# Sharing the first load of a 180-degree rotation between two DMA queues: by rows instead of by columns

## The chip, the cores and the metric

The kernel runs on one core of a Trainium2 chip. The metric is the time of one execution on the device in microseconds (us). The work is nearly all transfer: images are read from HBM into the core's SBUF (128 partitions), turned there by VectorE, and written back to HBM. Transfers are issued by an engine's instruction stream (SyncE or ACT here), each of which has a queue of its own, and are carried out by the core's 16 DMA engines.

## What is computed

```python
batch, c, h, w = 32, 3, 256, 256
x = np.random.randn(batch, c, h, w).astype(np.float32)

def reference(x):
    return np.rot90(x, k=2, axes=(-2, -1)).astype(np.float32)
```

Each of the 96 images is rotated by 180 degrees. Seen as one line of 65,536 numbers, an image is simply reversed. 25.17 MB are read and as many written.

## The kernel before

The 96 images are taken in three groups of 32. An image is cut into four quarters of E = 16,384 numbers (64 KB), and a group's 32 x 4 quarters are laid on the 128 partitions, one quarter to a partition. Row r of `x4[g]` is thus 64 KB that lie together in HBM, and goes to partition r. Three tiles `A`, `Bt` and `Ct` hold one group each, so that all three loads can be issued at once; a fourth, `T`, of J = 2,048 columns, is scratch.

The rotation has two parts. Within a quarter the numbers are reversed in SBUF by VectorE: `swap` (lines 61 to 65) exchanges a stretch of columns with its mirror image, by three copies, each of them reading backwards where needed: the right stretch into `T`, the left one to the right place, and `T` to the left place. `inside` (lines 67 to 69) does this for a whole tile in four swaps of 2,048 columns. The order of the four quarters of an image is reversed by the store (lines 57 to 59), which writes them in the order `::-1`. All copies are VectorE's, at line 52, held in program order.

What is issued, in order:

- The loads (line 55). `A`'s first 512 columns, 2 KB of each row, go on ACT's queue (line 72); its other 15,872 columns, 62 KB of each row, on SyncE's (line 73). Then SyncE issues the loads of `Bt` and `Ct`, 64 KB of each row (lines 74 and 75).
- VectorE turns `A` but for the middle: three swaps of 2,048 columns and one of 896 (lines 78 to 80). SyncE stores `A`'s first 128 columns, 64 KB in all (line 81).
- VectorE turns `Bt` (line 82), then the middle of `A`, 1,152 columns (line 83).
- SyncE stores the rest of `A` (line 84) and `Bt` (line 85). VectorE turns `Ct` (line 86), and SyncE stores it (line 87).

All stores and all loads but one are on SyncE's queue, where they are carried out in the order of issue. A semaphore for each transfer tells when it has landed; the waits are set by the framework from the regions that each instruction reads and writes. VectorE's first copy for a tile waits for its load, and SyncE's store waits for VectorE's last copy of what it stores.

Of the kernel before, what the change touches and what calls it, by code (L numbers as in the profile page):

```python
# [2 lines left out]

os.environ.setdefault("NEURON_RT_ULTRASERVER_MODE", "4")

# [4 lines left out]


@with_exitstack
def kernel(
    ctx: ExitStack,
    tc: tile.TileContext,
    x: bass.AP,
    out: bass.AP,
):

    nc = tc.nc
    P = 128

    B, C, H, W = x.shape
    L = H * W
    G = 32
    E = L // 4
    J = E // 8

    x4 = x.rearrange("b c h w -> (b c) (h w)").rearrange(
        "(g n) (s e) -> g (n s) e", n=G, s=4)
    o4 = out.rearrange("b c h w -> (b c) (h w)").rearrange(
        "(g n) (s e) -> g n s e", n=G, s=4)  # L40

    pool = ctx.enter_context(tc.tile_pool(name="slots", bufs=1))
    A = pool.tile([P, E], x.dtype, tag="A")
    Bt = pool.tile([P, E], x.dtype, tag="B")
    Ct = pool.tile([P, E], x.dtype, tag="C")
    T = pool.tile([P, J], x.dtype, tag="T")

    def back(t, lo, hi):
        return t[:, hi - 1:(lo - 1 if lo else None):-1]

    def copy(dst, src):
        tc.keep_in_program_order(nc.vector.tensor_copy(out=dst, in_=src))  # L52

    def load(t, g, lo, hi, queue=nc.sync):
        return queue.dma_start(out=t[:, lo:hi], in_=x4[g][:, lo:hi])  # L55

    def store(t, g, lo, hi):
        return nc.sync.dma_start(
            out=o4[g][:, ::-1, lo:hi], in_=t[:, lo:hi])

    def swap(t, lo, w):
        hi = E - lo - w
        copy(T[:, 0:w], back(t, hi, hi + w))
        copy(t[:, hi:hi + w], back(t, lo, lo + w))
        copy(t[:, lo:lo + w], T[:, 0:w])

    def inside(t):
        for lo in range(0, E // 2, J):
            swap(t, lo, J)

    HEAD = 512
    load(A, 0, 0, HEAD, nc.scalar)
    load(A, 0, HEAD, E)
    load(Bt, 1, 0, E)
    load(Ct, 2, 0, E)
    LAST = 1152
    LEAD = 128
    for lo in range(0, E // 2 - J, J):
        swap(A, lo, J)
    swap(A, E // 2 - J, J - LAST)  # L80
    store(A, 0, 0, LEAD)
    inside(Bt)
    swap(A, E // 2 - LAST, LAST)
    store(A, 0, LEAD, E)
    store(Bt, 1, 0, E)
    inside(Ct)
    store(Ct, 2, 0, E)


# [1 line left out]
_INS = ['x']  # L91
_OUTS = [((32, 3, 256, 256), 'float32')]


# [23 lines left out]
```

## Time and profile before

| | us |
|---|---|
| median of 3 runs | 121.94 (121.89 to 122.06) |
| the profiled execution | 122.03 |
| its span, from the first instruction to the last | 120.2 |
| VectorE (DVE) busy | 44.6, in 39 instructions |
| DVE's first copy starts | 22.68 |
| SyncE issues the large store of A | 59.62 |
| SyncE issues the store of Ct | 76.63 |

The profile of one execution gives, for each compute engine, its busy time, and a strip that cuts the span into 40 slices and shows each slice's busy share in tenths. Issuing a transfer isn't counted as busy. A row for each DMA queue says how many packets it carried, how many MB, and which share of the 16 DMA engines' time they took. A packet is what one DMA engine moves in one go; here it is one row of one transfer, and each transfer adds 16 packets of 4 bytes that signal its end. Times of an issue "to landing" run from the issuing instruction to the signal that all of it is there. Where a wait is listed, the engine, its tile and line stand first, then what ended the wait, the total, the number of times, and the longest.

### The profile page before, as it was taken

To read this page: it belongs to the slowest core of one execution; us is meant where nothing else is said; L and a number is where in the kernel's file an instruction comes from. 1 tells how busy PE (TensorE), PEld (TensorE's weight loads), DVE (VectorE), ACT (ScalarE), POOL (GpSimd) and SP (SyncE) were. 2 spreads that over 40 slices of the span, in tenths; PEclk is the share of its full clock that TensorE was granted. 3 is DMA by queue.
4 is the path that set the end of the run, shared out by engine and by line. 5 is a ranking of instruction groups with operands and counts; after the bars stand their busy time and mean duration, and the time that the engine had idled before them with its cause. 6 is when DMAs were issued, how large, how long until landed. Compare 5 with 4: busy or idle time off the path is not lost.

```text
span 120.2 us, 98 instructions
## 1 busy us (share of the span) xinstructions
DVE 44.6 (37%) x39; POOL 0.2 (0%) x4
## 2 busy tenths in 40 slices
DVE  0000000499990099999759999400000000000000
POOL 0000000000000000000000000000000000000000
DMA  9888988899889988998889777988898889888980
GB/s 338 349 349 349 698 349 349 360 654 392 349 349 610 436 349 349 589 458 349 349 368 692 346 346 346 692 349 349 349 698 349 349 349 698 349 349 349 676 371 0
DMA packets 1152, 50.33 MB, mean 419 GB/s; under 512 B 128, under 2 KB 256, under 8 KB 384
## 3 DMA queue, kind: packets, MB, share of 16 engines
q1 hardware_dynamic: 1008, 50.07, 96.7%
q10 hardware_dynamic: 144, 0.26, 0.6%
HBM read 25.17 MB, written 25.17 MB: 419 GB/s over the span
## 4 chain that ended last, share of the span: by engine, by line
DMA 34%; DVE 27%; another core or an unknown queue 2%; issue 1%; SPq 0%; DVEq 0%
DMA Bt<-in_x_dram 34%; DVE T L52 9%; DVE Bt L52 8%; DVE Ct L52 8%; DVE A L52 1%; SPq L55 0%; DVEq L52 0%
## 5 line engine op out<-in xcount | busy, mean ns | idle before, releaser
L52 DVE COPY T<-A 128x2048 f32<-128x2048 f32 (+2 forms) x5 | 5.1, 1014 | 22.8 <-DMA A<-in_x_dram 22.7
L52 DVE COPY T<-Bt 128x2048 f32<-128x2048 f32 x4 | 4.9, 1227 | 6.2 <-DMA Bt<-in_x_dram 6.1
L52 DVE COPY T<-Ct 128x2048 f32<-128x2048 f32 x4 | 4.9, 1227 | 2.0 <-DMA Ct<-in_x_dram 1.9
L52 DVE COPY A<-T 128x2048 f32<-128x2048 f32 (+2 forms) x5 | 5.1, 1013 | 0.2
L52 DVE COPY A<-A 128x2048 f32<-128x2048 f32 (+2 forms) x5 | 5.1, 1013 | 0.2
L52 DVE COPY Bt<-T 128x2048 f32<-128x2048 f32 x4 | 4.9, 1227 | 0.1
L52 DVE COPY Ct<-T 128x2048 f32<-128x2048 f32 x4 | 4.9, 1227 | 0.1
L52 DVE COPY Bt<-Bt 128x2048 f32<-128x2048 f32 x4 | 4.9, 1226 | 0.1
L52 DVE COPY Ct<-Ct 128x2048 f32<-128x2048 f32 x4 | 4.9, 1226 | 0.1
L102 POOL MEMSET const-bfloat16-1.0<- 128x1 bf16 x1 | 0.1, 103 | 0.0
L102 POOL MEMSET const-uint8-127<- 128x1 uint8 x1 | 0.1, 103 | 0.0
L102 POOL MEMSET const-float32-1.0<- 128x1 f32 x1 | 0.1, 100 | 0.0
L102 POOL MEMSET const-float32-0.0<- 128x1 f32 x1 | 0.1, 99 | 0.2 <-issue 0.2
## 6 DMA issues: line engine op xcount, KB each, us to landing
out_dram<-A SPq DMA_DIRECT2D x1, 8128.0 KB, 21.2
A<-in_x_dram SPq DMA_DIRECT2D x1, 7936.0 KB, 21.9
A<-in_x_dram ACTq DMA_DIRECT2D x1, 256.0 KB, 22.1
out_dram<-A SPq DMA_DIRECT2D x1, 64.0 KB, 35.2
Bt<-in_x_dram SPq DMA_DIRECT2D x1, 40.8
Ct<-in_x_dram SPq DMA_DIRECT2D x1, 59.8
out_dram<-Bt SPq DMA_DIRECT2D x1, 39.9
out_dram<-Ct SPq DMA_DIRECT2D x1, 42.8
```

The lines of the kernel that those rows point to most:

```text
L52: tc.keep_in_program_order(nc.vector.tensor_copy(out=dst, in_=src))
L102: nc = _bacc.Bacc("TRN2", target_bir_lowering=False, num_devices=1)
```

## The change

The two loads of `A` are cut in another way. Before, both touch all 128 rows: ACT's takes 2 KB of each row, SyncE's the other 62 KB. After, each takes 64 whole rows of 64 KB: SyncE's the even rows to the even partitions, ACT's the odd ones. SyncE's half stands first in the program. Nothing else differs.

```diff
-    HEAD = 512
-    load(A, 0, 0, HEAD, nc.scalar)
-    load(A, 0, HEAD, E)
+    SPLIT = 2
+    for i in range(SPLIT):
+        (nc.sync, nc.scalar)[i % 2].dma_start(
+            out=A[i::SPLIT, :], in_=x4[0][i::SPLIT, :])
     load(Bt, 1, 0, E)
     load(Ct, 2, 0, E)
```

## The prediction

> **What bounds the kernel now.** I read the page's strip of slices first, because it says at once whether an engine or the transfers set the time, then its queue table, then the issues with their landings, then the waits, and last the start of the span in small stretches.
>
> ```profile
> span 120.2 us, 98 instructions
> ...
> DVE 44.6 (37%) x39; POOL 0.2 (0%) x4
> ...
> DMA  9888988899889988998889777988898889888980
> ...
> q1 hardware_dynamic: 1008, 50.07, 96.7%
> q10 hardware_dynamic: 144, 0.26, 0.6%
> HBM read 25.17 MB, written 25.17 MB: 419 GB/s over the span
> ```
>
> VectorE (DVE) works 37% of the span, while the 16 DMA engines are busy in every slice but the last. q1 is SyncE's queue, q10 is ACT's. Together they hold the engines for 97.3% of the span, so about 3.2 us are left in which no transfer runs, most of them at the two ends: the first packet starts at 1.77 us, the last ends at 119.09. A change to the load can gain only by a cheaper packet, by an earlier first packet, or lose by opening a hole.
>
> ```profile
> A<-in_x_dram SPq DMA_DIRECT2D x1, 7936.0 KB, 21.9
> A<-in_x_dram ACTq DMA_DIRECT2D x1, 256.0 KB, 22.1
> ...
> Bt<-in_x_dram SPq DMA_DIRECT2D x1, 40.8
> Ct<-in_x_dram SPq DMA_DIRECT2D x1, 59.8
> ```
>
> The last column is the time from issue to landing. SyncE issues at 0.73, 1.18 and 1.65 us (timeline), so A is there at 22.8, Bt at 42.0 and Ct at 61.4: one group per 19.3 us, in a row, with nothing between. The packet records (each DMA packet's start and length) give the beat behind it. A 64 KB packet takes 2.418 us, and each engine starts the next one 2.4145 us after the last; a group is eight such rounds of 16 packets, 8 x 2.4145 = 19.32 us. In A's load a round is one 62 KB packet (2.342 us) and one 2 KB packet (0.084 us), and rounds follow at 2.419 us. The next two lines are the queue rows of the stretch from 4.75 to 7.15 us, one such round:
>
> ```profile
> q1 hardware_dynamic: 16, 1.02, 97.6%
> q10 hardware_dynamic: 16, 0.03, 3.5%
> ```
>
> Each engine takes one packet of SyncE's queue and one of ACT's in turn. That is why ACT's 256 KB, issued at 0.73, land only at 22.8 with the rest.
>
> The reader must also see who waits for A:
>
> ```profile
> DVE T L52 <- DMA A<-in_x_dram: 22.7, 1, 22.7
> DVE T L52 <- DMA Bt<-in_x_dram: 6.1, 1, 6.1
> DVE T L52 <- DMA Ct<-in_x_dram: 1.9, 1, 1.9
> ```
>
> Having finished its part of A, DVE waits 6.1 us for Bt. So A may land up to 6.1 us later and DVE is still in time for Bt. Behind Bt there is no such room: the chain from Bt's landing (42.0) through 12 copies of 1.23 us and three of 0.76 us ends at 59.6, the large store of A is issued at 59.62, and its first packets start at 60.82, when the first engines have just run out of loads (60.45) and of the eight 512-byte packets behind them (0.027 us each, so 60.7). Loads and this chain are level within 0.15 us. Both begin at the same place, the landing of the loads, so an earlier or later first round moves both and the end with them, one for one.
>
> **The change, part by part.**
>
> Bytes, issues and rounds. Two loads of A go (62 KB and 2 KB of each row), two come (64 whole rows each). SyncE still issues A, Bt, Ct and ACT one load, in parallel. Packets: 128 of 62 KB and 128 of 2 KB become 128 of 64 KB, half on each queue. Per engine that is 4 + 4 instead of 8 + 8. A round of A falls from 2.419 to 2.4145 us; over eight rounds -0.036 us. No work hides it, since the engines are the bound.
>
> Sharing. The round shown above alternates the queues packet by packet, so I take even, odd, even, odd on each engine, and A complete after eight rounds as now. If a queue ran ahead by a packet or two, A would land 2.4 to 4.8 us later, with Bt's first packets moved before it; Bt's end stays, because the bytes ahead of it are the same, and DVE's 6.1 us cover A. Cost nothing; without the cover it would be the excess over 6.1.
>
> DVE's first copy. It now needs both loads (before, only SyncE's; the second copy needed ACT's). Behind it stand all other copies, and SyncE's first store. A few hundredths of a us, covered by the same 6.1.
>
> The first round is the only term that could be seen. The stretches at the start (length, DVE, POOL, clock, DMA engines' share, GB/s booked where a packet starts):
>
> ```profile
> 1.50:2.00 0.50, 0.00 (x0) 0.00 (x0) 1.00 3.89 1270
> 2.00:2.50 0.50, 0.00 (x0) 0.00 (x0) 1.00 1.00 381
> 2.50:3.00 0.50, 0.00 (x0) 0.00 (x0) 1.00 0.90 381
> 3.00:4.75 1.75, 0.00 (x0) 0.00 (x0) 1.00 0.00 0
> ```
>
> 1270 GB/s over 0.5 us is ten packets of 62 KB, 381 is three. So ten engines begin by 2.0 us and the other six straggle to 2.89 us, while SyncE's issue has ended at 1.12. The early ten need 3.0 to 3.4 us for this packet, the late ones down to 2.34. All end between 4.78 and 5.27 us, and this spread of 0.49 us stays to the end of the loads (58.03 to 58.52 for the last round's starts). The slowest engine sets the landings, so what counts is the 5.27. Before, two loads of 128 rows are being turned into packets at that time; after it is two of 64, half the packets, and I guess that the six stragglers come from that work. The trace does not show it. Bounds: at best every engine ends its first packet at the earliest 4.78, -0.49 us. At worst the issue itself gets dearer: a load's issue takes 0.38 to 0.43 us, a store's, with its reordered rows, 0.54 to 0.63, so +0.25 us for rows with a step. I take the stragglers falling in with the early ten, whose last ends at 5.16: -0.11 us. It is the row nearest to the change, since nothing in it alters what the ten show.
>
> [...]
>
> Sum: -0.036 - 0.11 = -0.15 us. The profiled execution took 122.03 us, its span 120.2 and 1.8 around it; it becomes 121.88. It lies 0.09 above the median of the three runs (121.94), so against the median the forecast is 121.79, or **121.8 us**. About 0.2% (0.24 us) is what a measurement of this kernel can tell from no change, so the forecast is "the same".
>
> **The rivals.**
>
> *Faster, about 121.55.* The stragglers come wholly from the doubled packet work and the early ones' long first packets too; the first round ends near 4.9 us. -0.036 - 0.35 = -0.39 us. For it: the late six start while three further loads are being issued. Against it: 128 of the 256 packets removed are small, and Bt's and Ct's loads stay.
>
> *Slower: ACT's load waits for SyncE's, about 125.1.* Even and odd rows interleave in the same tile. If whoever sets the waits takes them for one overlapping region, ACT may issue only when the even rows have landed: 5.27 + 3 x 2.41 = 12.5, plus 0.4 until a wait is over (Bt: 41.6 last packet, 42.0 seen) and 1.0 from issue to first packet, 13.9. On each engine a Bt packet is then under way until 14.9; four odd ones alternating with three of Bt end at 14.9 + 7 x 2.41 = 31.8 instead of 22.3. DVE starts A 9.5 us later. 6.1 are covered, 3.4 are not: Bt's copies start at 45.5, A's last copy ends at 63.0, and its store's packets start at 64.2, when the engines have been out of work since 61.3. The end moves by about 3.2 us. It decides from the point where A is over 6.1 us late. Against it: before, the two parts of A's rows were kept apart rightly (both issue at 0.73).
>
> *Slower by the start, about 122.2.* The stepped rows make SyncE's and ACT's issue as dear as a store's, +0.25, with nothing won back.
>
> *The change doesn't do what it says: 64 rows don't fill 16 engines.* All transfers of the trace have 128 rows. Were a load of 64 rows to run at half the rate, A's eight rounds would last as long as sixteen, +19.3 us, 141.2. Against: 64 rows divide by 16 engines as 128 do. [...]
>
> **How the numbers follow.** Within 0.2%: 0.41, nearly all of it the forecast. Faster by more: 0.33, the first rival and the bound of the start. Slower by more: 0.26, made of 0.12 for a dearer or less lucky start, 0.10 for ACT's wait, 0.04 for half rate. The range takes in both bounds of the start: 121.94 - 0.036 - 0.49 = 121.41 and 121.94 + 0.25 = 122.19, each with about 0.1 more for the spread of the runs shown (121.89 to 122.06): 121.3 to 122.35. What it leaves out is the two dear cases, 0.14, and some chance beyond the ends.
>
> **What would show it.** In the profile after: 64 KB packets only in A's rounds, 8 on each queue in a round of 16, and rounds at 2.4145 us; ACT's issue still at 0.73 (if it is near 12.9, ACT waits); first packets all begun by about 2.5 us and ended by 5.16; A at about 22.6, Bt at 41.9; DVE's wait for Bt near 6.1. If A's rounds are longer than 2.42 us, the sharing of engines is wrong. If the first packets straggle as before or more, the term of the start is wrong, and only the 0.04 stands.

## The result and the profile after

The changed kernel takes 122.56 us (median of 9 runs, 122.27 to 123.07), the kernel before 122.00 in the runs beside it (9 runs, 121.89 to 122.32). The ratio is 1.0046, with a 95% interval from 1.003 to 1.0061: slower by about 0.56 us, clear of no change. The profiled execution took 122.66 us.

The page of the profile after, in the rows that were shown of before:

```profile
span 120.9 us, 97 instructions
...
DVE 44.6 (37%) x39; POOL 0.2 (0%) x4
...
DMA  8988998899889988998889877988898889888980
...
q1 hardware_dynamic: 944, 46.14, 88.3%
q10 hardware_dynamic: 80, 4.19, 8.5%
```

The picture is the same: the transfer engines are busy in all slices but the last, and VectorE does what it did. ACT's queue now carries 4.19 MB. The two queues hold 96.8% of a longer span; before it was 97.3%. In the packet records the last packet ends at 119.72 us instead of 119.09, so the 0.6 us lie before it. The timeline of the changed kernel shows where they begin (start, length, engine, line):

```profile
0.73 0.58 SPq L73 DMA_DIRECT2D A<-in_x_dram  x1
0.73 0.53 ACTq L73 DMA_DIRECT2D A<-in_x_dram  x1
1.36 0.81 SPq L55 DMA_DIRECT2D Bt<-in_x_dram  x1
2.21 0.44 SPq L55 DMA_DIRECT2D Ct<-in_x_dram  x1
```

The same issues before:

```profile
0.73 0.38 ACTq L55 DMA_DIRECT2D A<-in_x_dram  x1
0.73 0.39 SPq L55 DMA_DIRECT2D A<-in_x_dram  x1
1.18 0.43 SPq L55 DMA_DIRECT2D Bt<-in_x_dram  x1
1.65 0.43 SPq L55 DMA_DIRECT2D Ct<-in_x_dram  x1
```

The issues of A's halves have become dearer, that is longer, by 0.19 us on SyncE and 0.15 on ACT. The stretches at the start (the last column is GB/s, booked where a packet starts; a 64 KB packet in half a microsecond is 131):

```profile
1.50:2.00 0.50, 0.00 (x0) 0.00 (x0) 1.00 0.00 0
2.00:2.50 0.50, 0.00 (x0) 0.00 (x0) 1.00 4.69 1573
2.50:3.00 0.50, 0.00 (x0) 0.00 (x0) 1.00 0.75 262
3.00:3.50 0.50, 0.00 (x0) 0.00 (x0) 1.00 0.60 262
```

Where before ten engines began by 2.0 us, none does: twelve begin between 2.0 and 2.5, two in each stretch after it. By the packet records the first packet starts at 2.07 us (before 1.77), the last engine's first at 3.39 (2.89), and the slowest engine ends its first packet at 5.99 (5.27). Before, a 2 KB packet of 0.084 us still belonged to that round, so the slowest engine began its second round at 5.35, now at 5.99: 0.64 us later. From there on the delay is carried along:

```profile
DVE T L52 <- DMA A<-in_x_dram: 23.5, 1, 23.5
DVE T L52 <- DMA Bt<-in_x_dram: 5.8, 1, 5.8
DVE T L52 <- DMA Ct<-in_x_dram: 1.9, 1, 1.9
```

DVE gets A at 23.5 us instead of 22.7 and still waits 5.8 for Bt. Bt's copies start at 42.68 instead of 42.10, the large store of A is issued at 60.19 instead of 59.62, and the end is later by the same 0.6.

Sixteen packets of a stretch from 7.40 to 9.83 us, the third round, show the sharing, with ACT's queue first:

```profile
q10 hardware_dynamic: 16, 1.05, 99.6%
```

In the round before it all 16 were SyncE's, in the next they are again. Rounds of A follow at 2.416 us.

### The profile page after: what moved, and what is told of

The parts are those of the page before. It is cut to its first block, busy times and chain, and to the rows that moved or that the text cites. A ratio compares the mean times of both kernels' runs of the same rounds, so it can differ in the third digit from the quotient of the medians.

```text
span 120.9 us, 97 instructions
## 1 busy us (share of the span) xinstructions
DVE 44.6 (37%) x39; POOL 0.2 (0%) x4
## 3 DMA queue, kind: packets, MB, share of 16 engines
q10 hardware_dynamic: 80, 4.19, 8.5%
## 4 chain that ended last, share of the span: by engine, by line
DMA 34%; DVE 26%; another core or an unknown queue 1%; issue 1%; SPq 0%; DVEq 0%
DMA Bt<-in_x_dram 34%; DVE T L52 9%; DVE Bt L52 8%; DVE Ct L52 8%; DVE A L52 1%; SPq L73 0%; DVEq L52 0%
## 5 line engine op out<-in xcount | busy, mean ns | idle before, releaser
L52 DVE COPY T<-A 128x2048 f32<-128x2048 f32 (+2 forms) x5 | 5.1, 1014 | 23.7 <-DMA A<-in_x_dram 23.5
## 6 DMA issues: line engine op xcount, KB each, us to landing
A<-in_x_dram SPq DMA_DIRECT2D x1, 22.7
```

## The experiments

Two theories could stand after this profile. **STEP**: rows with a step between them are dear to turn into packets. **QUEUES**: two loads of equal weight on two queues hold each other up. A third, **ROWS**, that a load of 64 rows is dear for itself, is told apart by the first run. All kernels are edits of the kernel before unless said otherwise, and ratios are to it.

### e1_halves

```diff
-    load(A, 0, 0, HEAD, nc.scalar)
-    load(A, 0, HEAD, E)
+    nc.sync.dma_start(out=A[0:64, :], in_=x4[0][0:64, :])
+    nc.scalar.dma_start(out=A[64:128, :], in_=x4[0][64:128, :])
```

> SyncE loads rows 0 to 63 of A, ACT rows 64 to 127: 64 rows each as in the changed kernel, but without a step between rows. Theory STEP (rows with a step are dear to turn into packets): issues back at 0.38 to 0.43 us, first packets ended by 5.3 us, time 122.0. Theory ROWS (64 rows of 64 KB on each of two queues start late, stepped or not): issues at 0.53 to 0.58, first packets ended only near 6.0, time 122.5. [...]

Measured: 142.17 us, ratio 1.1659 [1.1643, 1.1675]. The start first, from the timeline of this run:

```profile
0.73 0.59 SPq L71 DMA_DIRECT2D A<-in_x_dram  x1
0.73 0.53 ACTq L72 DMA_DIRECT2D A<-in_x_dram  x1
1.37 0.80 SPq L55 DMA_DIRECT2D Bt<-in_x_dram  x1
```

There is no step between the rows, and the issues are as dear as in the changed kernel; the first packet starts at 2.07 us here too. STEP is out. Then the 20 us. The head and the queue row of a stretch from 6.7 to 11.6 us, one round of A:

```profile
DMA packets 16, 1.05 MB, mean 214 GB/s; under 512 B 0, under 2 KB 0, under 8 KB 0
...
q1 hardware_dynamic: 16, 1.05, 100.4%
```

All 16 engines work the whole stretch, at half the rate: a 64 KB packet takes 4.92 us instead of 2.42. A's rounds follow at 4.913 us, so the seven after the first cost 7 x (4.913 - 2.419) = 17.46 us more. The first ends 2.30 later (7.57 instead of 5.27), the late start included, and Bt's first packets still take 2.8 to 3.3 us. The slowest engine begins Bt's second round at 44.76 instead of 24.70, 20.06 us later, and the profiled executions differ by 20.03: that is the loss. From Bt's second round on, packets are back at 2.42. "64 rows don't fill the engines", one of the prediction's rivals with 19.3 us, is real for a block of rows and absent for every second row. e12_spread, below, finds on which side of the transfer it lies.

### e2_sync_only

```diff
-    load(A, 0, 0, HEAD, nc.scalar)
-    load(A, 0, HEAD, E)
+    load(A, 0, 0, E)
```

> SyncE loads A alone, in one load of 128 rows of 64 KB; ACT issues nothing. Theory STEP: a start like that of the kernel before, first packets ended by 5.3 us, 122.0. Theory QUEUES (two loads that are turned into packets at once hold each other up): a better start than the kernel before, first packets ended before 5.2, 121.8 or less.

Measured: ratio 1.0004 [0.9995, 1.0013], first issue 0.39 us, first packet at 1.75 (before 1.77). One load alone isn't measurably quicker to start than two, so the old 2 KB load on ACT neither helped nor harmed measurably, and QUEUES gets no support. The first packets have all ended only at 5.62 us, later than either theory expected. That is the profiled execution alone, which took 122.28 us, the longest of this kernel's eleven runs; their median is 122.04.

### e3_both_on_sync

```diff
-    load(A, 0, 0, HEAD, nc.scalar)
-    load(A, 0, HEAD, E)
+    for i in range(2):
+        nc.sync.dma_start(out=A[i::2, :], in_=x4[0][i::2, :])
```

> Even rows and odd rows as in the changed kernel, but both loads on SyncE, one behind the other. Theory STEP: issues of 0.53 us or more each, first packets ended near 6.0 us, 122.5. Theory QUEUES: the two no longer meet, issues back at about 0.4 us, first packets ended by 5.3, 122.0.

Measured: ratio 1.0042 [1.0029, 1.0055]; issues of 0.58 us each, first packet at 2.11 us, first packets ended by 5.65, between the two values expected. Without a second queue the loss is the same within the intervals. QUEUES falls.

### e4_columns

```diff
-    load(A, 0, 0, HEAD, nc.scalar)
-    load(A, 0, HEAD, E)
+    load(A, 0, 0, E // 2)
+    load(A, 0, E // 2, E, nc.scalar)
```

> SyncE loads columns 0 to 8191 of all 128 rows of A, ACT the other half: 32 KB of each row on each queue, no step, 128 rows. Theory STEP: issues of 0.38 us, first packets begun by 2.9 us, 122.0. Theory QUEUES in the form that two big loads of equal weight are worse than a big one and a small one: begun late, up to 3.4 us, 122.5.

Measured: ratio 1.0005 [0.9993, 1.0016]; issues 0.38 and 0.40, first packet at 1.74. Two queues with an equal share were no harm here, where each load has 128 rows.

What was left was ROWS, sharpened: the issue of a load of fewer than 128 rows takes longer, the first packet comes later by that and a little more, and nothing else is lost. If so, the loss must vanish where the dear issue lies under other transfers.

### e5_rows_behind

```diff
-    load(A, 0, 0, HEAD, nc.scalar)
-    load(A, 0, HEAD, E)
+    load(A, 0, 0, E // 2)
+    for i in range(2):
+        (nc.sync, nc.scalar)[i].dma_start(
+            out=A[i::2, E // 2:E], in_=x4[0][i::2, E // 2:E])
```

> SyncE loads the left half of A's columns for all 128 rows first; the right half follows by even rows on SyncE and odd rows on ACT. Theory ROWS (a load of 64 rows takes 0.2 us longer to issue and its packets start 0.3 us later; nothing else is dear about it): the 128-row load starts the engines at 1.75 us, the others are issued while they work, 122.0. Rival PACKETS (64-row loads cost in transit, by uneven engines or longer rounds): slower than before by 0.2 to 0.4%.

Measured: ratio 1.0000 [0.9988, 1.0012]. The issues of A's loads, from the timeline:

```profile
0.73 0.37 SPq L55 DMA_DIRECT2D A<-in_x_dram  x1
0.73 0.52 ACTq L73 DMA_DIRECT2D A<-in_x_dram  x1
1.16 0.56 SPq L73 DMA_DIRECT2D A<-in_x_dram  x1
```

The 64-row loads take 0.52 and 0.56 us to issue, as dear as ever, but the engines have begun at 1.73 us with the first load.

### e6_four

```diff
-    load(A, 0, 0, HEAD, nc.scalar)
-    load(A, 0, HEAD, E)
+    for i in range(4):
+        (nc.sync, nc.scalar)[i % 2].dma_start(
+            out=A[i::4, :], in_=x4[0][i::4, :])
```

> A by every fourth row: four loads of 32 rows, two on SyncE and two on ACT. ROWS with a cost for each load that isn't of 128 rows: first packets again at 2.07 us, so 122.5, not more, since the second load on each queue is issued under cover. Were the step between rows the cause, a step of four would be at least as dear, 122.5 or more.

Measured: ratio 1.0033 [1.0021, 1.0045]; first issues of 0.54 (ACT) and 0.58 us (SyncE), first packet at 2.06. Half as many rows and twice the step cost the same within the intervals, and only once.

### e7_rows_of_Bt

```diff
-    load(Bt, 1, 0, E)
+    for i in range(2):
+        nc.sync.dma_start(out=Bt[i::2, :], in_=x4[1][i::2, :])
```

> The kernel before, with Bt loaded by even and odd rows, both on SyncE, behind A. ROWS: Bt's two issues take 0.58 us each but lie under A's load, 122.0. PACKETS: the same 0.3 to 0.5% slower as with A's rows.

Measured: ratio 1.0006 [0.9997, 1.0014]. Bt's two issues take 0.56 and 0.60 us, under A's load. Bt's loads of even and of odd rows cost nothing measurable in transit.

### e8_later_loads

```diff
+    nc.vector.memset(Bt[:, 0:4096], 0.0)
     load(Bt, 1, 0, E)
```

> The kernel before, but VectorE first fills 4,096 columns of Bt with zeros (overwritten by the load), so that SyncE issues Bt and Ct only some 2 to 5 us into the span. If the six late engines at the start come from the issue of Bt and Ct, as the prediction guessed of the packet work, all first packets begin by 2.1 us and have ended by 5.1, and the time is 121.7. If not, the six stay late and the time is 122.0.

Measured: ratio 1.0011 [1.0002, 1.002]. Bt is now issued at 5.15 us, and the stretches of the start read:

```profile
1.50:2.00 0.50, 0.35 (x1) 0.00 (x0) 1.00 5.40 1778
2.00:2.50 0.50, 0.50 (x1) 0.00 (x0) 1.00 0.73 254
2.50:3.00 0.50, 0.50 (x1) 0.00 (x0) 1.00 0.00 0
```

Fourteen engines begin by 2.0 us and the other two by 2.5 (before: ten, three and three up to 2.89). In this profile the stragglers are gone with the issue of the next loads. That they come from it is not shown, though, since two later profiles speak against it. In e9_reordered Bt and Ct are issued at 1.43 and 2.04 us, and all 16 engines begin within 0.32 us; in e11_after_later Bt is issued at 5.15, and one engine begins only at 3.02. And nothing is won here: the first packets still end between 4.67 and 5.35 us (before 4.78 and 5.27), since each of the 16 takes 2.9 to 3.5 us, where the last four to begin took 2.34 to 2.49 before. The whole is slower by about 0.1%, barely clear of no change; the record doesn't say why.

### e9_reordered

```diff
-    load(A, 0, 0, HEAD, nc.scalar)
-    load(A, 0, HEAD, E)
+    x5 = x.rearrange("b c h w -> (b c) (h w)").rearrange(
+        "(g n) (s e) -> g n s e", n=G, s=4)
+    nc.sync.dma_start(out=A[:, :], in_=x5[0][:, ::-1, :])
```

> A in one load of 128 rows on SyncE, ACT issues nothing, but the four quarters of each image are read in reverse order, as the stores write them. The quarters of A's images end up in the order of the input, so the output is not the reference's for these 32 images. Theory ISSUE (whatever makes the first issue dear delays the first packet, and the end follows; the number of rows is only one such thing): issue 0.54 us or more, first packet at 2.05 us, 122.3. If only loads of less than 128 rows are dear: issue 0.39, first packet at 1.75, 122.0.

Measured: ratio 1.0031 [1.0019, 1.0042]. The first issue, from the timeline:

```profile
0.72 0.65 SPq L73 DMA_DIRECT2D A<-in_x_dram  x1
```

And the stretches of the start:

```profile
1.50:2.00 0.50, 0.00 (x0) 0.00 (x0) 1.00 0.00 0
2.00:2.50 0.50, 0.00 (x0) 0.00 (x0) 1.00 6.34 2097
```

The kernel beside it is e2_sync_only, the same one load with its rows in order: issue 0.39, first packet at 1.75, ratio 1.0004. One load of all 128 rows, on one queue, without a step that leaves rows out, loses 0.3% as soon as its issue is dear. No engine begins before 2.0 us, the first at 2.16, and A's rounds follow at 2.415 us, so nothing is lost behind the start. What the kernels that lose have in common is a long first issue and a late first packet; few rows are one way to get them. So ROWS becomes **ISSUE**.

### e10_head_first

```diff
     HEAD = 512
-    load(A, 0, 0, HEAD, nc.scalar)
-    load(A, 0, HEAD, E)
+    load(A, 0, 0, HEAD)
+    for i in range(2):
+        (nc.sync, nc.scalar)[i].dma_start(
+            out=A[i::2, HEAD:E], in_=x4[0][i::2, HEAD:E])
```

> SyncE first loads 512 columns of all 128 rows of A (2 KB of each), then the even rows of the rest; ACT loads the odd rows of the rest. ISSUE: the small load starts the engines at 1.75 us and keeps each busy for 8 x 0.084 = 0.67 us, longer than the 0.3 us that 64-row packets come late, so 122.0 to 122.1. If 64-row loads cost by something else, 122.4 to 122.6.

Measured: ratio 1.0002 [0.9994, 1.0011]. The issues of A's loads, from the timeline:

```profile
0.72 0.38 SPq L55 DMA_DIRECT2D A<-in_x_dram  x1
0.73 0.52 ACTq L74 DMA_DIRECT2D A<-in_x_dram  x1
1.17 0.57 SPq L74 DMA_DIRECT2D A<-in_x_dram  x1
```

The rows are shared as in the changed kernel, with the dear issues and all, but 256 KB of cheap issue stand in front, and their packets run from 1.73 us on. The loss is gone. This is the change, repaired; it is level with the kernel before and no better.

### e11_after_later

The edit is one of the changed kernel:

```diff
+    nc.vector.memset(Bt[:, 0:4096], 0.0)
     load(Bt, 1, 0, E)
```

> The changed kernel, with VectorE first filling 4,096 columns of Bt with zeros, so that SyncE issues Bt and Ct some 4.4 us later. ISSUE explains 0.31 us (first packet at 2.07 instead of 1.77) of the 0.56 lost. If the rest comes from Bt's issue (0.81 us in the changed kernel) falling into the first round, its ends come in from 5.99 to about 5.6 and the time is 122.3; if not, 122.55.

Measured: ratio 1.0039 [1.0026, 1.0053]; the slowest first packet ends at 5.83 us, between the two values expected, and the interval holds 1.0046, the ratio of the changed kernel. Whether Bt's issue of 0.81 us adds to the loss of the changed kernel is not settled by it.

### e12_spread

```diff
-    load(A, 0, 0, HEAD, nc.scalar)
-    load(A, 0, HEAD, E)
+    for i in range(2):
+        (nc.sync, nc.scalar)[i].dma_start(
+            out=A[i::2, :], in_=x4[0][64 * i:64 * (i + 1), :])
```

> Source as in e1_halves, destination as in the changed kernel: rows 0 to 63 of the group go by SyncE to the even partitions of A, rows 64 to 127 by ACT to the odd ones. The rows of the first 32 images are thereby exchanged among partitions, so their output is not the reference's. If the half rate of e1_halves comes from the partitions written (a block of 64 in SBUF), the rate is full again: rounds of 2.42 us and the changed kernel's time, 122.3 to 122.6. If it comes from the block of rows read in HBM, 142.

Measured: 122.35 us, ratio 1.0028 [1.0018, 1.0038]. 64 KB packets take 2.42 us in A's rounds. The rows are read from HBM as in e1_halves; only the partitions written differ. So the half rate of e1_halves, 4.92 us a packet and 214 GB/s over a round, comes from writing a block of 64 partitions. Why such a block is written at half the rate, no run shows.

## Why the prediction was wrong

It forecast 121.8 us, no change, as the likeliest case, with a gain as the next; the kernel became slower, and lies above the upper end of the range, 122.35.

- *What bounds the kernel; one for one.* Right. In the profile the slowest engine begins its second round 0.64 us later, Bt's copies begin 0.58 later, the last packet ends 0.62 later. The other profiles bear it out. By the packet records of before, after, e2, e6 to e9, e11 and e12, the last packet ends 113.65 to 113.75 us after the slowest engine has begun its second round (in e3, 113.96).
- *Bytes, issues and rounds, -0.036 us.* The rounds are right in kind and nearly nothing: 2.416 us, against 2.419 before and 2.4145 predicted. The issues were counted and their length put at nothing, which the first round shows to be wrong.
- *Sharing and DVE's first copy, 0.* Right in cost: the queues alternate, and DVE still waits 5.8 us for Bt. Two details differ. A round is all of one queue, 16 packets, ACT's first, and not 8 of each as the signs to look for had it. DVE's first copy comes 0.85 us later and not a few hundredths, which the 6.1 cover.
- *The first round, -0.11 us.* **This step failed, in its sign**: the slowest engine is done with its first round 0.64 us later, not 0.11 earlier. The step took the packet work as what the start waits for and halved it with the rows. The trace before had a row that warned: stores, whose rows are reordered, take 0.54 to 0.63 us to issue, loads 0.38 to 0.43, with 128 rows each. In the runs the cost of a queue's first issue went by the form of the transfer and not by its number of packets: 32 rows were as dear as 64 (0.54 and 0.58 us in e6_four, 0.53 and 0.58 in the changed kernel), and 128 reordered ones dearer still, 0.65 (e9_reordered). The prediction used the stores' row for its upper bound alone, and for a reason that is wrong, the step between rows. The runs give: as the first issue of a queue, 64 or 32 rows take 0.52 to 0.59 us, with or without a step (e1_halves, e6_four), and 128 plain rows 0.37 to 0.40.
- *The bound itself, +0.25 us, was too small.* It counted only the issue's length, and so the end of the range, which adds 0.16 to it, fell short too. By the profiles the first packet comes 0.29 to 0.39 us later for an issue 0.15 to 0.26 us longer, and the kernels with a dear first issue on A (the changed one, e3, e6, e9, e11, e12) lose 0.28 to 0.46%, 0.34 to 0.56 us. So the rival "slower by the start, 122.2" had the right place and the right cost, a dearer issue, though not for the step, at about half to three quarters of its price.
- *The stragglers.* The guess put them down to the packet work of A's two loads. With half the packets the last engine begins 1.32 us behind the first, before 1.12, so the guess does not hold, and neither does the -0.11 that rests on it. That the first round would end sooner without stragglers is wrong as well (e8_later_loads). What makes them stays open. The last sign of the prediction, that then only the 0.04 stands, left out the dearer issue.
- *ACT's wait.* Did not come: ACT issues at 0.73.
- *Half rate.* Not in this change, where 64 KB packets take 2.42 us, but waiting beside it: 4.92 us in e1_halves.

The cause is shown from both sides: a dear first issue without 64 rows loses (e9_reordered), and 64 rows without a dear first issue lose nothing (e5_rows_behind, e7_rows_of_Bt, e10_head_first). What stays open is up to 0.25 us of the changed kernel's 0.56. Its first packet is only 0.31 late; e12_spread, with the same issues and the same start, loses 0.28%, and the two intervals overlap. The end follows the slowest engine's first round, and that varies between profiles whose first packets start alike: the second round begins on it at 5.99 us in the changed kernel and at 5.62 in e12_spread, and at 5.62 behind the plain issue of e2_sync_only too. With one profile of each kernel this can't be told from chance. No run here says why a longer issue delays the first packet by more than its own length.

## What to carry to other kernels

In this kernel, whose transfers run from first to last with the two queues holding the engines for 97.3% of the span, the first issue was on the path (one of 0.65 us instead of 0.39 gave a ratio of 1.0031 instead of 1.0004, e9_reordered and e2_sync_only), and the dear ones that were tried behind a plain one were free (1.0000 to 1.0006 in e5_rows_behind, e7_rows_of_Bt and e10_head_first). For a kernel like it: begin with the plainest transfer there is, one of all 128 partitions with rows in order, and put the odd shapes behind it. Price a changed transfer from a row of the same form, not from its bytes or packets. The profile before had no load of 64 rows, but its stores showed that the length of an issue can differ with the form (0.54 to 0.63 us, loads 0.38 to 0.43). And don't cut a load into blocks of 64 partitions: in this kernel every second partition kept the rate, 2.42 us for a 64 KB packet, and a block halved it, 4.92.

## What the runs showed of the hardware that was not expected

- In e1_halves a block of 64 partitions was written at half the rate even though ACT's queue carried the other block at the same time: 4.92 us for a 64 KB packet on either queue. The engines took turns by whole rounds, all on one block and then all on the other.
- SyncE and ACT both issue at 0.73 us. With 128 rows on SyncE all 16 engines begin with SyncE's packets; in the changed kernel, e1_halves, e6_four, e11_after_later and e12_spread, where ACT's issue is 0.04 to 0.06 us shorter, all begin with ACT's.
- SyncE's issue of Bt, an unchanged load, takes 0.80 to 0.81 us straight behind a 64-row load that is each queue's first (the changed kernel, e1_halves, e12_spread), 0.57 to 0.61 as SyncE's third issue (e3_both_on_sync, e5_rows_behind, e6_four, e10_head_first) and 0.43 before. It lay under A's load; whether it costs anything was not settled (e11_after_later).
